# Inverses of 32x32 blocks: spread over partitions by VectorE's block transposes instead of through DRAM, in a bidirectional gated-DeltaNet encoder layer

## The chip, the cores and the metric

The kernel runs on one core of a Trainium2 chip. The metric is the device time of one execution in microseconds (us); lower is better. The kernel before took 1962.57 us, the median of three runs from 1961.55 to 1963.44.

## What is computed

One encoder layer over 16 learned ("meta") tokens and 1024 input tokens of width 1024, float32. A projection gives q, k, v, z and gates for eight heads. Branch A is a gated DeltaNet, run forward and backward in chunks; branch B is a short convolution. Both are gated, merged and projected, and a SwiGLU block follows. What matters here is the triangular system of each chunk, head and direction:

```
lmat = where(strict, beta[:, None] * (k @ k.T) * decay, 0)
a = lmat + eye
sol = triangular_solve(a, concat([v * beta, k * beta * exp(g)]), lower=True, unit_diagonal=True)
...
S = S * exp(g_last) + k_dec.T @ (u - w @ S)      # the scan over chunks
```

The kernel uses chunks of 128 tokens and builds the inverse of `a` itself: for each head 8 chunks in 2 directions, 16 matrices of 128x128. A small 16x16 system for the learned tokens comes on top.

## The kernel before, in words

**Stages.** The first stage (to about 985 us) does the input projection and, for each head, the whole DeltaNet branch. The second stage (from 985 us) does the other large products; the change does not touch it.

**Order in the first stage.** It is written out when the program is built. TensorE's main work are projection units: `dense_steps` (L332) multiplies 128 output columns by stretches of 320 to 512 tokens, 24 matmuls each, in groups of three. After each group `run_streams` and `pump` are called. They hold a simple clock for each engine (`T["pe"]`, `T["dve"]`, `T["act"]`, `T["pool"]`), to which `pe`, `V`, `A` and `on` add booked durations, for example `V(n)` = 68 + 1.042 n ns for VectorE and `A(n)` = 144 + 0.834 n ns for ScalarE. A stream is a Python generator that yields the time from which it may go on; it goes on when TensorE's clock has got there. So the pieces of the heads are put between the projection groups, and each engine then works its own instructions in this order. The streams of a head are `g_decay`, `g_norm` (norms of k and q, the scaled score matrices NP and PQ), `g_inv` (NP becomes its inverse) and `g_scan` (the recurrence over the chunks). Jobs of VectorE (convolutions, the substitution `fs_job`) lie in lanes that `pump` serves when VectorE's clock is free. `take` lets one of scan and inverse at a time use TensorE.

**The inverse, `g_inv`.** NP holds 16 matrices, chunk by chunk and direction by direction, rows on partitions. (1) The four 32x32 diagonal blocks `NP[B(b), c, d, B(b)]` are inverted by forward substitution, 64 blocks at once. For this each block shall lie in one partition row group: direction 1 is transposed in place (L639), the blocks are stored in DRAM (`nd`, L641) and loaded as `fN` (L653), one block row set per partition. `fP` starts as identity rows, GpSimd writes it. `fs_job` does 31 columns with two VectorE instructions each, a product into `tm` (L491) and a subtraction (L495). The result goes out to DRAM (`pd`, L671) and comes back into NP (L676). (2) Copies (L687 to L689) and transposes (L691 to L693, L697) prepare both forms of the inverted blocks, `X64` and `Xe`. (3) TensorE joins 32-wide blocks to 64-wide ones (L706, ScalarE's negated copy `T2` at L708, L714 and L716) and these to 128-wide ones (L729 and L730, `T3` at L732, L736 and L737).

**The learned tokens.** Their 16x16 matrix Nm (made in `g_norm`, L566 and L594) goes through DRAM to one partition (`mN`), GpSimd inverts it there (`mP`, L661 and L663) and the result goes through DRAM into `meta_inv` (L678), which the scan's first product uses.

**The scan's steps that are named below.** b1 and b2 are PSUM tiles: products with S (L796, L799), r from them on VectorE (L806), product with the inverse (L814), w on ScalarE (L821), state update S on VectorE (L841, L843).

**PSUM tiles.** Tag "m" (`psm`, 3 tiles) serves the projections, tag "e" (`psd`, 2 tiles) `g_norm`, tag "d" (`pss`, 3 tiles) inverse and scan. All DMAs of this stage are issued on SP's queue, in the order of the program.

Of the kernel before, what the change touches and what calls it, by code (L numbers as in the profile page):

```python
# [37 lines left out]
def encoder_layer(ctx: ExitStack, tc: tile.TileContext, x, meta, norm1_w, w_in,  # L38
# [183 lines left out]
    def pe(ns):  # L222
        T["pe"] += ns
        return T["pe"] + HOP
# [306 lines left out]
    def g_norm(h, st_):  # L531
# [90 lines left out]

    def g_inv(h, st_):

        NP, Nm = st_["NP"], st_["Nm"]

        nd = dr.tile([4, NC, 2, 32, 32], F32, tag="nd", name=uid("nd"), bufs=2)
        ndm = dr.tile([META, META], F32, tag="ndm", name=uid("ndm"), bufs=2)  # L630
        fN = dn.tile([P, 2, 512], F32, tag="fN", name=uid("fN")).rearrange("p a (j i) -> p (a j) i", i=32)
        fP = dn.tile([P, 16, 32], F32, tag="fP", name=uid("fP"))
        fPf = fP.rearrange("p j i -> p (j i)")
        mN = dn.tile([P, NC, 32], F32, tag="T2", name=uid("mN")).rearrange("p c i -> p (c i)")[:1]
        mPf = dn.tile([P, NC, 32], F32, tag="Xe", name=uid("mP")).rearrange("p c i -> p (c i)")[:1]
        mN, mP = (t.rearrange("p (j i) -> p j i", j=META) for t in (mN, mPf))
        nc.sync.dma_start(ndm, Nm)
        for b in range(4):
            nc.vector.transpose(NP[B(b), :, 1, B(b)], NP[B(b), :, 1, B(b)])  # L639
            on("dve", 467)  # L640
            nc.sync.dma_start(nd[b].rearrange("c d j i -> j (c d) i"),  # L641
                                             NP[B(b), :, :, B(b)].rearrange("j c d i -> j (c d) i"))
        nc.gpsimd.memset(fP, 0.0)
        nc.gpsimd.memset(fPf[0:64, 0:8 * 33:33], 1.0)
        nc.gpsimd.memset(fPf[0:64, 8 * 32 + 24:512:33], 1.0)
        nc.gpsimd.memset(fPf[64:128, 8:512:33], 1.0)
        nc.gpsimd.memset(mP, 0.0)
        nc.gpsimd.memset(mPf[:, 0:256:17], 1.0)
        on("pool", 500)
# [7 lines left out]
        for j in range(META - 1):  # L657
            n = META - 1 - j
            tm = dn.tile([1, 64], F32, tag="tmm", name=uid("tm"), bufs=1)
            tv = tm[:, :(j + 1) * n].rearrange("p (r i) -> p r i", r=j + 1)  # L660
            nc.gpsimd.tensor_tensor(out=tv, in0=mP[:, 0:j + 1, j:j + 1].broadcast_to([1, j + 1, n]),  # L661
                                    in1=mN[:, j:j + 1, j + 1:META].broadcast_to([1, j + 1, n]), op=ALU.mult)
            nc.gpsimd.tensor_tensor(out=mP[:, 0:j + 1, j + 1:META], in0=mP[:, 0:j + 1, j + 1:META], in1=tv,  # L663
                                    op=ALU.subtract)
            yield max(on("pool", 700) - TOPE, T["pe"] + 500)
        while not job.done:
            yield T["pe"] + 100
        yield T["dve"] + HOP
        pd = dr.tile([4, NC, 2, 32, 32], F32, tag="pd", name=uid("pd"), bufs=2)
        for r, src in (((0, 8), fP[0:64, 0:8]), ((24, 32), fP[0:64, 8:16]), ((8, 24), fP[64:128])):  # L670
            nc.sync.dma_start(pd[:, :, :, r[0]:r[1]].rearrange("b c d j i -> d (b c) (j i)"), src.rearrange("p j i -> p (j i)"))  # L671
# [1259 lines left out]
```

## Time and profile before

| | before |
|---|---|
| timed runs, median (lowest to highest) | 1962.57 us (1961.55 to 1963.44) |
| profiled execution: span from its first to its last instruction | 1959.4 us |
| time of the profiled execution around the span | not listed by itself; the median lies 3.2 us above the span |
| TensorE busy | 1941.7 us, 99% of the span |
| VectorE, ScalarE, GpSimd busy | 1468.1, 867.9, 158.4 us |
| mean granted TensorE clock | 0.999 |
| first stage, last projection matmul | near 985 us |

Busy time of TensorE comes from matmul records that overlap, with modelled ends, so 99% means that hardly a gap is seen, not that it runs at its peak. An instruction's name in the profile is line, engine, operation, output<-inputs and shape. Idle time carries the name of what ended it.

### The profile page before, as it was taken

To read this page: it belongs to the slowest core of one execution; us is meant where nothing else is said; L and a number is where in the kernel's file an instruction comes from. 1 tells how busy PE (TensorE), PEld (TensorE's weight loads), DVE (VectorE), ACT (ScalarE), POOL (GpSimd) and SP (SyncE) were. 2 spreads that over 40 slices of the span, in tenths; PEclk is the share of its full clock that TensorE was granted. 3 is DMA by queue.
4 is the path that set the end of the run, shared out by engine and by line. 5 is a ranking of instruction groups with operands and counts; after the bars stand their busy time and mean duration, and the time that the engine had idled before them with its cause. 6 is when DMAs were issued, how large, how long until landed. Compare 5 with 4: busy or idle time off the path is not lost.

```text
span 1959.4 us, 31938 instructions
## 1 busy us (share of the span) xinstructions
PE 1941.7 (99%) x11962; PEld 1704.4 (87%) x11962; DVE 1468.1 (75%) x2804; ACT 867.9 (44%) x2014; POOL 158.4 (8%) x457
## 2 busy tenths in 40 slices
PE   8999999999999999999999999999999999999998
PEld 8998899999899999998888888887888888888887
DVE  4778778788887888787358798559787887756574
ACT  5463544646455554533445545234232332324343
POOL 3012112020110202110000000000000000000001
PEclk9999999999999999999999999999999999999999
DMA  4222332323222222224386623332666644587654
GB/s 146 68 76 80 103 99 60 87 60 87 60 76 67 85 65 79 70 69 153 103 310 246 206 88 121 115 119 73 212 232 209 209 165 163 179 279 243 194 181 155
DMA packets 243136, 264.11 MB, mean 135 GB/s; under 512 B 46820, under 2 KB 166933, under 8 KB 240549
## 3 DMA queue, kind: packets, MB, share of 16 engines
q1 hardware_dynamic: 242981, 262.07, 42.1%
q8 instruction: 94, 1.54, 0.3%
q14 instruction: 61, 0.50, 0.1%
HBM read 189.58 MB, written 72.44 MB: 134 GB/s over the span
## 4 chain that ended last, share of the span: by engine, by line
PE 89%; DVE 5%; ACT 3%; issue 1%; DMA 1%; POOL 0%; SPq 0%; POOLq 0%; DVEq 0%; ACTq 0%
PE pm L332 31%; PE pm L1382 5%; PE pd L1382 4%; PE pe L1382 3%; PE pm L1656 3%; PE pm L1658 3%; PE pm L1657 2%; PE pd L1658 2%; PE pd L1656 2%; PE pd L1657 2%; PE pe L1658 2%; PE pe L1656 2%; PE pe L1657 2%; PE pm L1814 1%; PE pm L1815 1%; PE pm L1813 1%
## 5 line engine op out<-in xcount | busy, mean ns | idle before, releaser
L332 PE MATMUL pm<-hTh,wh 128*128 128x512 f32 (+4 forms) x1328 | 483.8, 365 | 0.1
L332 PE MATMUL pm<-hTh,wl 128*128 128x512 f32 (+4 forms) x1328 | 450.5, 340 | 0.0
L332 PE MATMUL pm<-al,wh 128*128 128x512 f32 (+4 forms) x1328 | 449.6, 339 | 0.5 <-DVE al L1047 0.5
L332 PEld LDWEIGHTS pm<-hTh,wl 128*128 128x128 f32 x1328 | 249.1, 188 | 15.5
L332 PEld LDWEIGHTS pm<-hTh,wh 128*128 128x128 f32 x1328 | 250.2, 189 | 13.6 <-ACT hTh L1041 0.2
L332 PEld LDWEIGHTS pm<-al,wh 128*128 128x128 f32 x1328 | 250.4, 189 | 12.9 <-DVE al L1047 0.7
L87 DVE TENSOR_TENSOR al<-raw,ring_h 128x1024 fp32r<-128x1024 f32 x73 | 88.4, 1223 | 63.6 <-ACT ring_h L86 63.2
L86 ACT CAST ring_h<-raw 128x1024 fp32r<-128x1024 f32 x73 | 76.9, 1054 | 109.7 <-PE pd L1815 35.3
L940 DVE TENSOR_TENSOR wl<-raw,wh 128x512 fp32r<-128x512 f32 x122 | 84.1, 690 | 32.0 <-ACT wh L943 27.1
L355 DVE SCALAR_TENSOR_TENSOR kq<-ra,wc,kq 128x520 f32<-128x520 f32 (+1 forms) x128 | 95.9, 749 | 2.3 <-ACT kq L389 1.2
L821 ACT ACTIVATE w<-pd,small 128x128 f32<-128x128 f32 x128 | 40.2, 365 | 124.9 <-PE pd L814 106.4
L128 POOL TENSOR_SCALAR ss<-ss 128x1 f32<-128x1 f32 x13 | 4.6, 353 | 951.1 <-ACT b L1825 603.4
L491 DVE TENSOR_TENSOR tm<-fP,fN 128x135 f32<-128x135 f32 (+23 forms) x248 | 72.1, 291 | 10.0 <-DMA fN<-nd 3.3
L495 DVE TENSOR_TENSOR fP<-fP,tm 128x135 f32<-128x135 f32 (+23 forms) x248 | 71.8, 289 | 7.3
L943 ACT CAST wh<-raw 128x512 fp32r<-128x512 f32 x122 | 74.8, 619 | 0.1
L87 DVE TENSOR_TENSOR raw<-pair,raw 128x1024 fp32r<-128x1024 f32 (+1 forms) x42 | 48.0, 1143 | 30.4 <-ACT raw L86 30.4
L86 ACT CAST raw<-pair 128x1024 fp32r<-128x1024 f32 (+1 forms) x42 | 41.7, 992 | 58.4 <-PE pd L1382 27.5
L87 DVE TENSOR_TENSOR wl<-pair,wh 128x1024 fp32r<-128x1024 f32 (+1 forms) x42 | 48.1, 1144 | 21.7 <-ACT wh L86 21.6
L86 ACT CAST wh<-pair 128x1024 fp32r<-128x1024 f32 (+1 forms) x42 | 41.7, 992 | 46.0 <-PE pd L1382 24.7
L843 DVE SCALAR_TENSOR_TENSOR S<-S,eGl,pd 128x128 f32<-128x128 f32 x104 | 31.8, 344 | 38.2 <-PE pd L831 30.8
L130 POOL TENSOR_TENSOR small<-small,minus_half 128x9 f32<-128x9 f32 x16 | 29.5, 1842 | 353.8 <-DVE small L878 264.0
L661 POOL TENSOR_TENSOR tm<-mP,mN 1x15 f32<-1x15 f32 (+7 forms) x120 | 37.3, 311 | 237.0 <-DMA mN<-ndm 228.7
(660 smaller groups left out, 4945.7 us busy)
## 6 DMA issues: line engine op xcount, KB each, us to landing
raw<-in_w_in_dram SPq DMA_DIRECT2D x64, 512.0 KB
raw<-in_w_gate_up_dram SPq DMA_DIRECT2D x44, 512.0 KB
sums<-in_w_down_dram SPq DMA_DIRECT2D x22, 512.0 KB
t_d<-sums SPq DMA_DIRECT2D x11, 1024.0 KB
raw<-s_d SPq DMA_DIRECT2D x44, 256.0 KB
raw<-t_d SPq DMA_DIRECT2D x44, 256.0 KB
act_d<-b SPq DMA_DIRECT2D x43, 256.0 KB
raw<-act_d SPq DMA_DIRECT2D x33, 256.0 KB
```

Source lines behind the costliest of these rows:

```text
L86: nc.scalar.copy(hi, src)
L87: nc.vector.tensor_tensor(out=lo, in0=src, in1=hi.bitcast(F32), op=ALU.subtract)
L332: mm(po[:, :n], (wl if j == 2 else wh)[:, k], xl[k][:, t0:t0 + n] if j == 1 else xh[k][:, t0:t0 + n], start=(i == 0), stop=(i == 3 * KT - 1))
L355: nc.vector.scalar_tensor_tensor(out=acc, in0=raw[:, h0 + t:h0 + t + hn], scalar=wc[:, t, col:col + 1], in1=acc, op0=ALU.mult, op1=ALU.add)
L491: nc.vector.tensor_tensor(out=tv, in0=fP[:, 0:r, j:j + 1].broadcast_to([P, r, n]), in1=fN[:, j:j + 1, j + 1:32].broadcast_to([P, r, n]), o ...
L495: nc.vector.tensor_tensor(out=fP[:, 0:r, j + 1:32], in0=fP[:, 0:r, j + 1:32], in1=tv, op=ALU.subtract)
L940: nc.vector.tensor_tensor(out=u[1][1][:, k], in0=u[2][:, k], in1=u[1][0][:, k].bitcast(F32), op=ALU.subtract)
L943: nc.scalar.copy(u[1][0][:, k], u[2][:, k])
L1382: mm(bank[t], a[:, c], b, start=fresh, stop=first and k == 3 and j == 2, skip_group_check=not first)
L1656: mm(po, ah[:, k], bhk, start=k == 0, stop=False)
L1657: mm(po, ah[:, k], blk, start=False, stop=False)
L1658: mm(po, al[:, k], bhk, start=False, stop=k == 3)
```

## The change

- **Spread.** ScalarE copies the four diagonal blocks of NP into a PSUM tile E of tag "e" (L657). VectorE transposes the 32x32 blocks of one direction in E (L660, 128x256), and then E as a whole into `fN` (L662, 128x1024, each block twice). No DRAM.
- **Substitution.** A partition now holds every second row of its block: `r = j // 2 + 1` rows are worked on at column j. GpSimd writes the new identity pattern with ten memsets.
- **Back.** VectorE transposes `fP` into Z (L674) and Z into W (L677), 128x512 each; they are both forms of the inverted blocks. TensorE's first products read them, and ScalarE copies the blocks into NP (`diag`) and `X64` later, between the products.
- **Learned tokens.** A stream of its own, `g_meta`, starts as soon as Nm is scaled. Nm (now with its sign turned) goes out to DRAM once and comes back to 16 partitions, all 16 rows in each; GpSimd then works one row of the inverse per partition, directly in `meta_inv`. The scan waits for `inverted` and `learned`.

The diff without the renaming in the third step:

```diff
@@ fs_job
-            r = min(j + 1, 8) if j < 16 else 8 + min(j - 15, 8)
+            r = j // 2 + 1
@@ g_norm
-        nc.vector.tensor_scalar(out=Nm, in0=Nm, scalar1=cc[:META, 8, 0:1], scalar2=None, op0=ALU.mult)
+        nc.vector.tensor_scalar(out=Nm, in0=Nm, scalar1=cc[:META, 8, 0:1], scalar2=-1.0, op0=ALU.mult, op1=ALU.mult)
         on("dve", 950)
+        st_["Nm_done"] = True
@@ new stream
+    def g_meta(h, st_):
+        Nm = st_["Nm"]
+        ndm = dr.tile([META, META], F32, tag="ndm", name=uid("ndm"), bufs=2)
+        mN = dn.tile([P, META, META], F32, tag="mN", name=uid("mN"))[:META]
+        nc.sync.dma_start(ndm, Nm)
+        yield T["dve"] + LAND
+        nc.sync.dma_start(mN, ndm.unsqueeze(0).broadcast_to([META, META, META]))
+        Pm = st_["Pm"] = meta_inv[h % 2]
+        mP = Pm[:META, :META]
+        nc.gpsimd.tensor_copy(mP, ident[:META, :META])
+        yield T["pe"] + 5600
+        for j in range(META - 1):
+            tm = dn.tile([META, META], F32, tag="tmm", name=uid("tm"))[:, j + 1:]
+            nc.gpsimd.tensor_scalar(out=tm, in0=mN[:, j, j + 1:], scalar1=mP[:, j:j + 1], scalar2=None, op0=ALU.mult)
+            nc.gpsimd.tensor_tensor(out=mP[:, j + 1:], in0=mP[:, j + 1:], in1=tm, op=ALU.add)
+            yield max(on("pool", 500) - TOPE, T["pe"] + 400)
@@ g_inv, spread
-        nc.sync.dma_start(ndm, Nm)
         for b in range(4):
-            nc.vector.transpose(NP[B(b), :, 1, B(b)], NP[B(b), :, 1, B(b)])
-            on("dve", 467)
-            nc.sync.dma_start(nd[b].rearrange("c d j i -> j (c d) i"), NP[B(b), :, :, B(b)].rearrange("j c d i -> j (c d) i"))
-        yield T["dve"] + LAND
-        for s in range(2):
-            for d in range(2):
-                nc.sync.dma_start(fN[64 * s + 32 * d:64 * s + 32 * d + 32], nd[:, :, d].rearrange("b c j i -> (b c) j i"))
-        nc.sync.dma_start(mN, ndm.unsqueeze(0))
-        yield T["pe"] + 5600
+            nc.scalar.copy(E[B(b)].rearrange("p d c i -> p c d i"), NP[B(b), :, :, B(b)])
+            A(512)
+        yield T["act"] + HOP
+        nc.vector.transpose(E[:, 0], E[:, 0])
+        yield V(256) - TOPE + DEP
+        nc.vector.transpose(fN.rearrange("p i (s x) -> p i s x", s=2),
+                            E.rearrange("p d c i -> p i (d c)").unsqueeze(2).broadcast_to([P, 32, 2, 2 * NC]))
+        yield V(1024) - TOPE + DEP
         job = enqueue("fs", fs_job(h, fN, fP))
-        ... (the learned tokens' 15 steps on one partition)
@@ g_inv, back
-        for r, src in (((0, 8), fP[0:64, 0:8]), ((24, 32), fP[0:64, 8:16]), ((8, 24), fP[64:128])):
-            nc.sync.dma_start(pd[...], src.rearrange("p j i -> p (j i)"))
-        nc.sync.dma_start(pdm.unsqueeze(0), mP)
-        yield T["dve"] + LAND
-        for b in range(4):
-            nc.sync.dma_start(NP[B(b), :, :, B(b)].rearrange("j c d i -> j (c d) i"), pd[b].rearrange("c d j i -> j (c d) i"))
-        nc.sync.dma_start(Pm[:META, :META], pdm)
-        yield T["pe"] + 5600
+        nc.vector.transpose(Z.rearrange("p d c r -> p r (d c)"), fP.rearrange("p r (s x) -> p (r s) x", s=2))
+        yield V(512) - TOPE + DEP
+        nc.vector.transpose(W, Z)
+        yield V(512) + HOP - TOPE
         yield from take("inv")
-        ... (three copies and seven transposes of 32x256)
+        def diag(d, b):
+            nc.scalar.copy(NP[B(b), :, d, B(b)], rows_[d][B(b), d])
+            A(256)
         ... (first products)
+        for d, b in ((0, 2), (0, 3), (1, 0), (1, 1)):
+            diag(d, b)
         yield t
         nc.scalar.mul(T2, pt, -1.0)
         ... (products with T2; after them four copies into X64, four from pp into NP as before, two diag)
         ... (64-wide products, T3, two diag, products with T3 as before)
@@ g_scan
-        while not st_.get("inverted"):
+        while not (st_.get("inverted") and st_.get("learned")):
```

Three places show what moves. Names end in buffer numbers: pe_, pd_ and pm_ are PSUM tiles of the tags "e", "d" and "m", kq_64 is head 1's k and q.

First, TensorE at the end of head 0's scores, where head 1's normalisation begins; before:

```order
L332 MATMUL pm_145_1533<-al_3_128,wh_118_1298 128x384
L332 MATMUL pm_145_1533<-hTh1_130,wl_119_1299 128x384
L83 MATMUL pe_155_1595<-ident_70,kq_64_896 128x128
L557 MATMUL pe_155_1595<-kq_64_896 128x16
L83 MATMUL pe_156_1598<-ident_70,kq_64_896 128x128 x4
L332 MATMUL pm_162_1614<-hTh0_129,wh_135_1443 128x512
```

And now:

```order
L332 MATMUL pm_151_1550<-al_3_128,wh_118_1298 128x384
L332 MATMUL pm_151_1550<-hTh1_130,wl_119_1299 128x384
L83 MATMUL pe_166_1632<-ident_70,kq_64_896 128x128
L557 MATMUL pe_166_1632<-kq_64_896 128x16
L83 MATMUL pe_167_1635<-ident_70,kq_64_896 128x128 x4
L332 MATMUL pm_174_1653<-hTh0_129,wh_137_1448 128x512
```

TensorE's order is the same, but between the last score tile and pe_166 a tile of the same tag, pe_160 (E), has been handed out.

Second, ScalarE at that place; before:

```order
L388 COPY ra_141_1492<-pm_142_1496 128x320
L389 ACTIVATE kq_123_1336<-pm_142_1496,wc_154 128x320
L561 COPY kn_154_1594<-pe_155_1595 128x128
L545 ACTIVATE jk_157_1604,small_153_1592<-pe_155_1595 16x128
L388 COPY ra_141_1492<-pm_145_1533 128x384
```

And now:

```order
L388 COPY ra_143_1497<-pm_144_1501 128x320
L389 ACTIVATE kq_123_1336<-pm_144_1501,wc_154 128x320
L657 COPY pe_160_1609<-NP_127_1353 32x8x2x32 x4
L561 COPY kn_165_1631<-pe_166_1632 128x128
L545 ACTIVATE jk_168_1641,small_164_1629<-pe_166_1632 16x128
L360 ACTIVATE rb_170_1645<-vT_65_897 128x520
```

The four copies into E stand ahead of the copy that reads pe_166.

Third, VectorE between head 0's substitution and its first products; before, after the trip through DRAM:

```order
L473 SCALAR_TENSOR_TENSOR rb_279_2284<-rb_279_2284,pm_275_2241 128x512
L363 SCALAR_TENSOR_TENSOR kq_123_1336<-rb_278_2276,kq_123_1336 128x520
L691 STREAM_TRANSPOSE XT_277_2260<-NP_127_1353 32x8x32
L692 STREAM_TRANSPOSE XT_277_2260<-NP_127_1353 32x8x32
L693 STREAM_TRANSPOSE Xe_276_2259<-NP_127_1353 32x256
L697 STREAM_TRANSPOSE NP_127_1353<-NP_127_1353 32x8x32 x4
```

And now, three instructions after the last substitution step:

```order
L495 TENSOR_TENSOR fP_162_1611<-fP_162_1611,tm_277_2191 128x16
L355 SCALAR_TENSOR_TENSOR kq_123_1336<-ra_125_1338,wc_154,kq_123_1336 128x520
L939 TENSOR_TENSOR wl_262_2131<-raw_236_1959,wh_261_2130 128x512
L674 STREAM_TRANSPOSE XT_278_2199<-fP_162_1611 128x32x16
L355 SCALAR_TENSOR_TENSOR kq_123_1336<-ra_125_1338,wc_154,kq_123_1336 128x520
L677 STREAM_TRANSPOSE W_283_2223<-XT_278_2199 128x512
```

Seven short transposes behind a DMA have become two long ones in a chain (the second reads what the first wrote), close behind the substitution.

More of the change, by code (lines that the diff above doesn't have):

```diff
@@ L654, in g_inv @@
-        nc.sync.dma_start(mN, ndm.unsqueeze(0))
-        yield T["pe"] + 5600
-        job = enqueue("fs", fs_job(h, fN, fP))
[L657 to L665, printed above, removed]
+        fPf = fP.rearrange("p r i -> p (r i)")
@@ L672, in g_inv @@
-        pdm = dr.tile([META, META], F32, tag="pdm", name=uid("pdm"), bufs=2)
-        nc.sync.dma_start(pdm.unsqueeze(0), mP)
-        yield T["dve"] + LAND
-        for b in range(4):
-            nc.sync.dma_start(NP[B(b), :, :, B(b)].rearrange("j c d i -> j (c d) i"), pd[b].rearrange("c d j i -> j (c d) i"))
-        Pm = st_["Pm"] = meta_inv[h % 2]
-        nc.sync.dma_start(Pm[:META, :META], pdm)
-        Xe = dn.tile([P, NC, 32], F32, tag="Xe", name=uid("Xe"))
         XT = dn.tile([P, 2, 512], F32, tag="fN", name=uid("XT"))
-        X64 = XT[:, 0].rearrange("p (c i) -> p c i", c=NC)
+        Z = XT[:, 0].rearrange("p (d c i) -> p d c i", d=2, c=NC)
@@ L955, in start_streams @@
             nnorm += 1
+        h = nmeta
+        if h < H and not metas and heads[h].get("Nm_done"):
+            metas.append([g_meta(h, heads[h]), T["dve"] + HOP, h])
+            nmeta += 1
         h = ninv
@@ L971, in run_streams @@
             again = False
-            for q in (scans, invs, norms, decs):
+            for q in (scans, invs, metas, norms, decs):
                 if q and q[0][1] <= T["pe"]:
```

93 lines of the change are left out of this document (42 added, 51 removed).

## The prediction

> **What bounds the kernel now.** I read the page first (busy shares), then the windows of the two stages, then TensorE's own waits, then the timeline around each of these waits. The first rows are the page's span and TensorE row, and two rows of the windows: columns are the stretch, its length, and busy time of PE, PEld, DVE, ACT and POOL, then the granted clock, the DMA share and GB/s.
>
> ```profile
> span 1959.4 us, 31938 instructions
> PE 1941.7 (99%) x11962; PEld 1704.4 (87%) x11962; DVE 1468.1 (75%) x2804; ACT 867.9 (44%) x2014; POOL 158.4 (8%) x457
> 100.00:900.00 800.00, 796.14 (x6554) 742.04 (x6553) 655.32 (x1707) 413.00 (x1322) 120.42 (x364) 1.00 0.29 78
> 985.00:1959.40 974.40, 965.69 (x4320) 799.55 (x4318) 712.53 (x895) 369.48 (x468) 15.61 (x33) 1.00 0.55 186
> ```
>
> TensorE is busy 796.14 of 800 us where all eight inversions run, at full clock. Every long step of a head is covered by projection matmuls (L332), which are put into the gaps. So the DRAM trips that the change removes cost nothing by their length: a head may wait 20 us and TensorE goes on. The change can gain only where TensorE itself stood still for an inversion, and lose only where it will. These are its waits (what, for whom: total us, times, longest):
>
> ```profile
> PE pd L714 <- ACT T L708: 1.7, 1, 1.7
> ...
> PE pd L796 <- DVE S L843: 0.6, 1, 0.6
> ...
> PE pd L814 <- DVE r L806: 0.5, 2, 0.3
> ...
> PE pd L729 <- POOL small L130: 0.4, 1, 0.4
> ```
>
> Idle time understates a wait, since a matmul's modelled end covers its first part. I take waits from starts instead: a matmul of 512 columns starts 0.23 us after the last, one of 384 columns 0.18 us, and the first small one of an interlude 0.32 us after a 512-column one when nothing is late (first two rows). The next rows are the same kind of place in other heads.
>
> ```profile
> 201.86 0.39 PE L332 MATMUL pm<-hTh,wl 128*128 128x512 f32 x1
> 202.18 0.21 PE L714 MATMUL pd<-NP,T 32*32 32x32 f32 x1
> ...
> 491.34 0.34 PE L332 MATMUL pm<-hTh,wl 128*128 128x384 f32 x1
> 493.35 0.21 PE L714 MATMUL pd<-NP,T 32*32 32x32 f32 x1 [1.67 <-ACT T L708]
> ...
> 702.99 0.34 PE L332 MATMUL pm<-hTh,wl 128*128 128x384 f32 x1
> 703.76 0.30 PE L729 MATMUL pd<-XT,NP 64*64 64x64 f32 x2 [0.43 <-POOL small L130]
> 704.21 0.24 PE L730 MATMUL pd<-XT,NP 64*64 64x64 f32 x1 [0.16 <-POOL fP L643]
> ...
> 233.45 0.40 PE L332 MATMUL pm<-hTh,wl 128*128 128x512 f32 x1
> 234.42 0.75 PE L796 MATMUL pd<-S,kq 128*128 128x128 f32 x4 [0.57 <-DVE S L843]
> ...
> 236.61 0.40 PE L332 MATMUL pm<-hTh,wl 128*128 128x512 f32 x1
> 237.32 0.71 PE L814 MATMUL pd<-r,NP 128*128 128x128 f32 x4 [0.32 <-DVE r L806]
> ```
>
> At 491 the step took 2.01 us against 0.27 (0.32 less the 0.05 by which 384 columns are shorter): 1.7 us lost. At 703 it is 0.77 - 0.27 = 0.5, and 0.4 more between L729 and L730, which start together elsewhere: 0.9. At 233 and 237 it is 0.97 - 0.23 = 0.74 and 0.71 - 0.23 = 0.48: 1.2. The first two (2.6 us) stand inside the inversion. The other two stand in a scan, and VectorE's timeline says why:
>
> ```profile
> 226.37 0.61 DVE L806 SCALAR_TENSOR_TENSOR r<-pd,negEG,vS 128x128 f32<-128x128 f32 x2 [1.46 <-PE pd L796]
> 230.28 0.22 DVE L491 TENSOR_TENSOR tm<-fP,fN 128x31 f32<-128x31 f32 x1 [3.30 <-DMA fN<-nd]
> ...
> 233.76 0.34 DVE L495 TENSOR_TENSOR fP<-fP,tm 128x135 f32<-128x135 f32 x1
> 234.03 0.59 DVE L843 SCALAR_TENSOR_TENSOR S<-S,eGl,pd 128x128 f32<-128x128 f32 x2
> ```
>
> VectorE stood 3.30 us in front of the first substitution step, because fN had not come back from DRAM. The scan's state update S (L843) queued behind it and came late, and with it the products that wait for S and r. This is the one place where the removed round trip reaches TensorE.
>
> **The change part by part.** *DMAs.* Of 19 transfers a head on SP's queue (Nm out, four nd, four fN, mN, three pd, pdm, four into NP, meta_inv) two stay, Nm out and a broadcast mN: 136 fewer in all. Nothing on TensorE waits for a DMA in this stage, so only the 1.2 us at 233 and 237 comes back, and weight loads behind them on SP come sooner, which nothing waits for.
>
> *VectorE.* Prices (mean ns of one is the number behind the comma):
>
> ```profile
> L697 DVE STREAM_TRANSPOSE NP<-NP 32x256 f32<-32x256 f32 x32 | 13.9, 435 | 1.2 <-ACT Xe L687 0.4
> L491 DVE TENSOR_TENSOR tm<-fP,fN 128x144 f32<-128x144 f32 x16 | 5.0, 310 | 0.4
> L491 DVE TENSOR_TENSOR tm<-fP,fN 128x16 f32<-128x16 f32 x8 | 1.5, 182 | 0.3
> L141 DVE TENSOR_TENSOR pair<-pair,pair 128x1024 f32<-128x1024 f32 x30 | 35.8, 1218 | 1.0 <-DMA pair<-in_w_branch_dn_dram 0.8
> ```
>
> An element costs (310 - 182) / 128 = 1.0 ns. The substitution keeps its 62 instructions a head, but r * n summed over the 31 columns falls from 3752 to 2856, so two passes save 1.8 us. Eleven transposes of 0.435 us (4.8 us) become four: 256 elements 0.44, 1024 elements 1.22, two of 512 at 0.70 (between the two rows), 3.1 us in all. Together 3.5 us a head, 28 us of the 655 above. VectorE is no bound; this is slack, and I book no time for it. No row shows a transpose that writes with a stride of 32 elements as the third one does: between 0.70 and, if such writes halve the rate, 1.4 us. I take 0.70 (the 32x256 rows lie on the same line as ordinary instructions) and keep 1.4 for the slow rival.
>
> *ScalarE.* It gains 13 instructions a head: four copies of 32x512 into PSUM, four of 32x256 into X64, eight of 32x256 back into NP, less three. By these rows that is 4 * 0.58 + 12 * 0.41 - 3 * 0.41 = 6.0 us a head, 48 on 413 busy of 800: room enough.
>
> ```profile
> L687 ACT COPY Xe<-NP 32x256 f32<-32x256 f32 x8 | 3.2, 406 | 9.5 <-DMA NP<-pd 6.4 <-DMA meta_inv<-pdm 3.0
> L739 ACT COPY NP<-pd 64x512 f32<-64x512 f32 x8 | 4.6, 581 | 14.3 <-PE pd L737 14.3
> ```
>
> *GpSimd* keeps 30 small instructions for the learned tokens and gets ten short memsets. They start earlier, in a job of their own, and end before the inverse; VectorE's first substitution step waits for the memsets. I book nothing; if the transfer of mN were as late as fN was at 230, the price would be that 1.2 us once.
>
> *TensorE* has the same matmuls, and the order shows as many interludes between projection matmuls (342 before, 343 after): no term.
>
> *The wait that is added.* The inversion's copy target E takes one of two PSUM tiles of the tag "e" from head 0's last score product until the second transpose. In that stretch head 1's normalisation starts: pe_166 gets the other tile, and the token transposes into the next tile (L83) must wait until ScalarE and VectorE have read pe_166. On ScalarE the four E copies stand ahead of this reading. The same place before:
>
> ```profile
> 130.63 0.27 PE L83 MATMUL pe<-ident,kq 128*128 128x128 f32 x1
> 130.74 0.29 PE L557 MATMUL pe<-kq 128*128 128x16 f32 x2
> 130.88 0.64 PE L83 MATMUL pe<-ident,kq 128*128 128x128 f32 x4
> ...
> 128.43 0.60 DVE L613 SCALAR_TENSOR_TENSOR NP<-pe,small,PQ 128x128 f32<-128x128 f32 x2
> ...
> 131.06 0.27 ACT L561 COPY kn<-pe 128x128 f32<-128x128 f32 x1 [4.23 <-PE pe L557]
> 131.23 0.26 ACT L545 ACTIVATE jk<-pe 16x128 f32<-16x128 f32 x1
> 131.40 0.18 ACT L545 ACTIVATION_READ_ACCUMULATOR jk<-pe 16x1 f32 x1
> ...
> 132.79 0.16 DVE L566 TENSOR_TENSOR Nm<-pe,Dm 16x16 f32<-16x16 f32 x1
> ```
>
> The last scores are written at 129.03 and the E copies can start there; ScalarE is idle for 4.23 us. Four of 0.58 that overlap a little end near 131.2. Then the copy of kn, the square with its reading (to about 131.7) and Nm (0.16 and a hand-over): the tile is free near 131.9, and TensorE, which started at 130.88, stands 1.0 us. Below, with ScalarE free when pe_166 is ready, the reading ends at 131.58 and Nm at 131.8: 0.9. Above, copies without overlap end at 131.5 and a projection step of VectorE stands in front of Nm: 1.6. I take 1.0, once.
>
> The Trainium skill (Perfetto Trace Analysis, Optimization Strategy) says that the same gap returning on the engine that should be saturated can mean that there is too little PSUM for the next tile. By it the gap would come in each of eight heads: 8.0 instead of 1.0 and a time near 1968. In the order I find matmuls into tag "e" only inside head 0's E; the trace of before, without E, has no such gap.
>
> *New steps on the inverse's way.* TensorE meets it four times a head as before (first products, products with T2, 64-wide products, products with T3). But the first now follow the substitution directly, behind two chained transposes, and on ScalarE copies stand ahead of T2 and T3. The planner books 601 ns for a 512-element transpose (68 + 1.042 * 512) where 0.70 us is to be expected, and 357 ns for a copy that takes 406: some 0.1 to 0.3 us late a head against a margin of 0.2 to 0.4. Before, six of eight heads lost nothing and two lost 1.7 and 0.9. Bounds: 0 a head, and 0.9 in each (7.2). I take 0.2 a head, 1.6, nearest to the six.
>
> **Sum.** -2.6 (inversion's waits) - 1.2 (fN late) + 1.0 (E) + 1.6 (new steps) = -1.2 us. The profiled span is 1959.4; the three timed runs lie around 1962.57, 3.2 above it, which I take as unchanged: 1961.4 us. The measurement tells about 0.2% (3.9 us) from no change, so this is "same", with a range of its own of 1959.5 to 1964.
>
> **Rivals.**
> 1. *Slower: the DRAM trips were slack.* The planner gave each trip 5.5 us and more, in which a late VectorE caught up. Now a late substitution hits TensorE at once, and if strided transposes take 1.4 us, the two make the first products 0.7 to 1.4 us late in every head. For it: the planner's price is under the rows. Against: TensorE's row shows scan steps that hang on VectorE with similar margins, and only 0.6 and 0.5 us of waits on them. At 1.4 a head: -3.8 + 1.0 + 11.2 = +8.4, 1971. It decides (+3.9) from 0.85 us a head. Chance 0.14. The E gap in every head (1968) has 0.03.
> 2. *Faster.* VectorE is 28 us freer and the new steps fit their margins: -3.8, only part of 1.0, and some small waits of the scans go too: 1958, from 1959 down to 1956.5. Against: TensorE's whole idle time in that stage is 3.9 us. Chance 0.15.
> 3. *Nothing moves*: the trips were covered, ScalarE's lateness at 491 comes back elsewhere as it does not hang on the inverse's transport: 1962.6. Chance 0.13.
>
> **Chances.** The forecast 0.55. Same by 0.2% holds it and the third rival, 0.68; faster 0.15, slower 0.17. The range reaches to the whole faster case and to the start of the slow one, where 0.14 is left out above and little below: 1957.5 to 1967.
>
> **What would show it.** No fN, nd or pd rows, and no DMA wait in front of L491; STREAM_TRANSPOSE x32 of four lengths, 512 elements at about 0.70 us; VectorE's busy time in 100 to 900 us near 627, ScalarE's near 460; one wait of about 1 us on TensorE near 131 us at L83 behind L566. Rival 1 would show waits at L692 on W in most heads; the tag "e" rule, a wait at L83 or L583 in each. I am wrong if the waits at L692, L703, L725 and L735 add up to over 6 us, or if the scans' waits go altogether.

## The result, and the profile after

The changed kernel takes 1983.95 us (median, 1983.25 to 1983.99), the kernel before 1963.01 us on the same chip: 1.0107 times as long, with a 95% interval from 1.0092 to 1.0121. I had forecast 1961.4. The change costs 21 us, and TensorE's instruction count is what it was.

The page of the changed kernel, and the windows' row that answers to the 796.14 of before:

```profile
span 1982.3 us, 31711 instructions
PE 1948.3 (98%) x11962; PEld 1708.7 (86%) x11962; DVE 1440.5 (73%) x2748; ACT 913.0 (46%) x2118; POOL 167.5 (8%) x497
100.00:900.00 800.00, 779.99 (x6463) 727.52 (x6462) 618.60 (x1637) 456.26 (x1423) 129.56 (x404) 0.99 0.21 63
```

VectorE's and ScalarE's totals came out near the forecast (618.6 against 627, 456.3 against 460), yet TensorE is busy for 16 us less of the same 800. The first stage's last projection matmul (L332) starts at 1007.2 us instead of 985.2, and the rest of the program takes 975.1 us against 974.2: almost all of the loss lies in the first stage. Its waits there (what, for whom: total us, times, longest):

```profile
PE pe L83 <- DVE Nm L566: 9.4, 5, 6.2
PE pd L692 <- DVE XT L674: 2.7, 1, 2.7
PE pd L692 <- DVE W L677: 1.8, 2, 0.9
PE pd L813 <- DVE r L805: 1.7, 2, 1.0
PE pd L83 <- DVE NP L898: 1.5, 1, 1.5
...
PE pd L795 <- DVE S L784: 0.8, 1, 0.8
PE pd L703 <- issue: 0.6, 1, 0.6
PE pd L726 <- ACT XT L708: 0.5, 1, 0.5
```

Measured from starts as in the prediction (each interlude, that is, what stands between two projection groups, against the shortest of its kind; places over 0.06 us), before loses 10.4 us in 35 places and the changed kernel 29.0 in 46. I call this sum "lost in waits" below. It is a guide and no exact account: it leaves out projection matmuls that run at a slow clock, and it can miss a wait in an interlude that has no second one of its kind. Here it explains 18.6 of the 22 us. Two places hold 11 us, 131 (6.7) and 491 (4.3); the others have at most 1.7.

**At 131 us.** This is the place where I had forecast one wait of 1.0 us behind E. The timeline, of GpSimd (POOL), ScalarE and TensorE:

```profile
131.97 0.26 ACT L561 COPY kn<-pe 128x128 f32<-128x128 f32 x1
132.12 0.30 POOL L638 TENSOR_SCALAR tm<-mN,meta_inv 16x8 f32<-16x8 f32 x1
...
134.67 0.51 POOL L649 MEMSET fP<- 128x512 f32 x1
...
136.81 0.18 POOL L539 MEMSET small<- 128x108 f32 x1
...
137.02 0.27 ACT L545 ACTIVATE jk<-pe 16x128 f32<-16x128 f32 x1 [4.80 <-POOL small L539]
...
137.53 0.16 DVE L566 TENSOR_TENSOR Nm<-pe,Dm 16x16 f32<-16x16 f32 x1 [5.96 <-ACT jk L545]
...
137.75 1.11 PE L83 MATMUL pe<-ident,kq 128*128 128x128 f32 x4 [6.18 <-DVE Nm L566]
```

Read from the bottom: TensorE waits for Nm, Nm (on VectorE) for the square, the square (on ScalarE, 4.80 us) for a memset of head 1's "small". That memset is GpSimd's, and it stands behind head 0's learned-token steps and fP's ten memsets. Before, the same L539 ran at 124.86. A pair of steps is booked with 500 ns; in the trace head 0's follow each other at 0.66 to 1.31 us, and at 2.14 where fP's memsets come between.

The wait has a second price. In the windows of this stretch the number behind POOL's busy time is the granted clock:

```profile
134.00:136.00 2.00, 0.00 (x0) 0.00 (x0) 0.00 (x0) 0.00 (x0) 1.62 (x11) 1.00 0.00 0
136.00:138.00 2.00, 0.25 (x1) 0.26 (x2) 0.47 (x2) 0.97 (x4) 1.54 (x8) 0.61 0.00 0
138.00:140.00 2.00, 2.00 (x8) 1.60 (x8) 1.97 (x4) 0.86 (x3) 0.65 (x3) 0.50 0.00 0
142.00:144.00 2.00, 2.00 (x12) 1.74 (x11) 0.00 (x0) 0.88 (x3) 0.00 (x0) 0.68 0.00 0
144.00:146.00 2.00, 2.00 (x13) 1.69 (x12) 0.00 (x0) 1.85 (x9) 0.00 (x0) 1.00 0.00 0
```

TensorE comes back at half its clock and keeps it for some 5.5 us; a 512-column matmul takes 0.43 us from start to start there instead of 0.23, and about 2.5 us more are lost (an estimate from these steps).

**At 491 us** the substitution ends late and the first products wait for both transposes:

```profile
488.80 0.16 DVE L566 TENSOR_TENSOR Nm<-pe,Dm 16x16 f32<-16x16 f32 x1 [3.26 <-ACT jk L545]
...
492.66 1.04 DVE L674 STREAM_TRANSPOSE XT<-fP 128x512 f32<-128x512 f32 x1
...
493.75 0.25 PE L692 MATMUL pd<-XT,NP 32*32 32x32 f32 x4 [2.74 <-DVE XT L674]
494.16 0.69 DVE L677 STREAM_TRANSPOSE W<-XT 128x512 f32<-128x512 f32 x1
...
494.91 0.26 PE L692 MATMUL pd<-W,NP 32*32 32x32 f32 x2 [0.91 <-DVE W L677]
```

VectorE had stood 3.26 us in front of Nm of the head after, which waited for ScalarE, and the last substitution steps stood behind Nm.

**At 388 us** ScalarE's queue shows plainly. A block of the inverse's copies stands ahead of the next head's kn:

```profile
385.10 0.81 ACT L708 COPY XT<-XT 32x256 f32<-32x256 f32 x2
...
385.93 0.81 ACT L708 COPY XT<-W 32x256 f32<-32x256 f32 x2
...
386.76 1.49 ACT L715 COPY NP<-pd 32x256 f32<-32x256 f32 x4
...
388.26 0.81 ACT L686 COPY NP<-XT 32x256 f32<-32x256 f32 x2
389.10 0.27 ACT L561 COPY kn<-pe 128x128 f32<-128x128 f32 x1
...
389.98 0.65 PE L83 MATMUL pe<-ident,kq 128*128 128x128 f32 x4 [1.31 <-DVE Nm L566]
```

### The profile page after: what moved, and what is told of

Same layout as the page of the kernel before. It is cut to its first block, busy times and chain, and to the rows that moved or that the text cites. A ratio compares the mean times of both kernels' runs of the same rounds, so it can differ in the third digit from the quotient of the medians.

```text
span 1982.3 us, 31711 instructions
## 1 busy us (share of the span) xinstructions
PE 1948.3 (98%) x11962; PEld 1708.7 (86%) x11962; DVE 1440.5 (73%) x2748; ACT 913.0 (46%) x2118; POOL 167.5 (8%) x497
## 4 chain that ended last, share of the span: by engine, by line
PE 81%; DVE 9%; ACT 6%; issue 1%; DMA 1%; POOL 1%; SPq 0%; POOLq 0%; ACTq 0%; DVEq 0%
PE pm L332 26%; PE pm L1385 4%; PE pd L1385 4%; PE pe L1385 3%; PE pm L1659 2%; PE pm L1661 2%; PE pm L1660 2%; PE pd L1661 2%; PE pd L1660 2%; PE pd L1659 2%; PE pe L1661 2%; PE pe L1660 2%; PE pe L1659 2%; PE pm L1817 1%; PE pm L1818 1%
## 5 line engine op out<-in xcount | busy, mean ns | idle before, releaser
L332 PE MATMUL pm<-hTh,wh 128*128 128x512 f32 (+4 forms) x1328 | 485.5, 366 | 0.1
L332 PE MATMUL pm<-hTh,wl 128*128 128x512 f32 (+4 forms) x1328 | 451.0, 340 | 0.0
L332 PE MATMUL pm<-al,wh 128*128 128x512 f32 (+4 forms) x1328 | 450.2, 340 | 0.5 <-DVE al L1050 0.5
L332 PEld LDWEIGHTS pm<-hTh,wl 128*128 128x128 f32 x1328 | 249.8, 188 | 15.7
L332 PEld LDWEIGHTS pm<-hTh,wh 128*128 128x128 f32 x1328 | 250.9, 189 | 13.6 <-ACT hTh L1044 0.2
L332 PEld LDWEIGHTS pm<-al,wh 128*128 128x128 f32 x1328 | 251.1, 189 | 13.1 <-DVE al L1050 0.7
L355 DVE SCALAR_TENSOR_TENSOR kq<-ra,wc,kq 128x520 f32<-128x520 f32 (+1 forms) x128 | 95.7, 748 | 1.4
L128 POOL TENSOR_SCALAR ss<-ss 128x1 f32<-128x1 f32 x13 | 4.6, 350 | 975.1 <-ACT b L1828 603.4
L495 DVE TENSOR_TENSOR fP<-fP,tm 128x126 f32<-128x126 f32 (+22 forms) x248 | 62.8, 253 | 6.9
L491 DVE TENSOR_TENSOR tm<-fP,fN 128x126 f32<-128x126 f32 (+22 forms) x248 | 62.8, 253 | 6.7
L870 ACT ACTIVATE jk<-NP 128x128 f32<-128x128 f32 x64 | 19.9, 310 | 82.5 <-DVE NP L866 82.1
```

Source lines behind the costliest of these rows:

```text
L332: mm(po[:, :n], (wl if j == 2 else wh)[:, k], xl[k][:, t0:t0 + n] if j == 1 else xh[k][:, t0:t0 + n], start=(i == 0), stop=(i == 3 * KT - 1))
L355: nc.vector.scalar_tensor_tensor(out=acc, in0=raw[:, h0 + t:h0 + t + hn], scalar=wc[:, t, col:col + 1], in1=acc, op0=ALU.mult, op1=ALU.add)
L491: nc.vector.tensor_tensor(out=tv, in0=fP[:, 0:r, j:j + 1].broadcast_to([P, r, n]), in1=fN[:, j:j + 1, j + 1:32].broadcast_to([P, r, n]), o ...
L495: nc.vector.tensor_tensor(out=fP[:, 0:r, j + 1:32], in0=fP[:, 0:r, j + 1:32], in1=tv, op=ALU.subtract)
```

## The experiments

Each row is one kernel: its median, its ratio to the kernel before on the same chip with the interval, where its last L332 starts, and what it lost in waits. The last two columns are read from the one profiled execution, which can lie some us from the median (e8's took 1981.8).

| kernel | us | ratio | last L332 | lost |
|---|---|---|---|---|
| before (first chip) | 1963.0 | 1 | 985.2 | 10.4 |
| changed | 1984.0 | 1.0107 [1.0092, 1.0121] | 1007.2 | 29.0 |
| e1 small by VectorE | 1977.7 | 1.0078 [1.0063, 1.0093] | 999.8 | 23.3 |
| e2 learned tokens only | 1966.5 | 1.0020 [1.0011, 1.0029] | 989.9 | 13.3 |
| e4 blocks only | 1978.1 | 1.0077 [1.0060, 1.0094] | 1002.6 | 24.3 |
| e3 e1 + measured prices | 1971.6 | 1.0045 [1.0030, 1.0060] | 994.1 | 17.2 |
| e5 e3 + E copies one by one | 1979.6 | 1.0091 [1.0076, 1.0106] | 1001.4 | 21.0 |
| e6 e3 + T2 first | 1979.2 | 1.0090 [1.0075, 1.0105] | 1000.8 | 21.5 |
| e7 e5 + e6 + E in tag d | 1975.2 | 1.0071 [1.0054, 1.0087] | 997.5 | 19.6 |
| e8 e3 + diagonals on VectorE | 1978.0 | 1.0088 [1.0073, 1.0103] | 1004.2 | 20.6 |
| d1 e1 without diagonals | 1972.2 | 1.0052 [1.0037, 1.0067] | 994.8 | 17.7 |
| d3 e1, contiguous | 1976.5 | 1.0079 [1.0063, 1.0096] | 999.3 | 21.0 |
| d4 d1 + d3 | 1970.5 | 1.0046 [1.0031, 1.0061] | 993.7 | 16.3 |
| v1 e1, half of E on VectorE | 1986.1 | 1.0126 [1.0109, 1.0143] | 1009.8 | 30.6 |
| s1 e3 + slack | 1967.1 | 1.0027 [1.0016, 1.0038] | 990.5 | 12.0 |
| s3 s1 without diagonals | 1964.6 | 1.0014 [1.0005, 1.0024] | 988.0 | 10.6 |
| s2 s1 + T2 first, tag d | 1969.8 | 1.0040 [1.0025, 1.0055] | 993.5 | 16.7 |
| p1 before, LAND 5300 | 1959.0 | 0.9985 [0.9975, 0.9994] | 984.5 | 9.4 |
| p3 before, LAND 5700 | 1957.7 | 0.9980 [0.9971, 0.9989] | 981.0 | 6.0 |
| p5 before, LAND 6500 | 1959.9 | 0.9991 [0.9982, 1.0001] | 983.8 | 7.2 |

**GpSimd's queue (e1, e2, e4).** e1 moves one memset:

```
-        nc.gpsimd.memset(small, 1.0)
+        nc.vector.memset(small, 1.0)
```

> The changed kernel with one memset moved: 'small' of each head (L539) is set by VectorE instead of GpSimd. Theory A (GpSimd's queue): at 131 us ScalarE's square (L545) stood 4.80 us for this memset, which was queued behind the learned tokens' 30 steps and the ten memsets of fP; TensorE stood 6.7 us, and then ran some 5 us at a granted clock of 0.50 (another 2.5 us). Then the wait at L83 near 131 us shrinks to about 1.3 us, the slow clock there goes, and the time falls by 7 to 9 us, to about 1976. Rival B (ScalarE's four E copies hold the tile, the memset was only the last to come): the wait stays above 4 us and the time above 1981. Neither touches the stall of 4.3 us at 491.

6.3 us faster, a little less than the 7 to 9 of theory A, with every other instruction where it stood. At 131 1.4 us are lost instead of 6.7, and the slow clock there is gone. The row for all five heads falls from 9.4 us, longest 6.2, to

```profile
PE pe L83 <- DVE Nm L566: 4.5, 5, 1.4
```

So GpSimd's queue carries 6.3 of the 21 us, and the wait that the prediction gave E is 1.4. (One gap grew, from 0.6 to 2.0 us, near 270; it is explained under e3.) e2 and e4 apply one half of the change each: e2 is g_meta with its job (L627 to L640) on the old g_inv, e4 the new g_inv with the old one-partition steps.

> The kernel before with the learned tokens' part of the change alone (own job, one row per partition on GpSimd; its row of mN is kept as a packed triangle to fit the memory, in two DMAs); the blocks go through DRAM as before. Theory A: the steps stand in GpSimd's queue ahead of the next head's memset of 'small' here too, so head 1's L83 waits several us and the time rises by 5 to 9 us, to 1968 to 1972. If the learned tokens' part only hurts together with the fP memsets and the E copies, the time stays at 1962 to 1964 and the blocks' part carries the 21 us.

> The changed kernel's blocks (E, block transposes, new substitution) with the learned tokens as before: one partition, inside the inversion's job, through DRAM and back. Theory A: no GpSimd steps run beside the next head's normalisation, so no long wait near 131 us: 1972 to 1977. Theory C and D: the waits of the inversion and of the scans are there as in the changed kernel, 8 to 12 us above the kernel before. If the blocks' part is harmless by itself, 1962 to 1964.

e2 costs about 4 us (theory A said 5 to 9): its only new wait of weight is L83 at 133, 3.4 us lost, behind the same memset at 135.53, and its clock, too, is at 0.50 behind it (136.2 to 139.6 us). e4 costs 15.5 us, above what any theory expected, and has no long wait at 131 (1.4 us lost). The two halves add up to 19.5 of the 21 us, but each half is also a new order of the instructions, which by itself moves the time (e5 to e8 below), so the sum proves little.

**What the planner books (e3), and its order (e5 to e8).**

```
-            A(512)                              # E copies, 571
+            on("act", 605)
-        yield V(512) - TOPE + DEP               # L674, 601
+        yield on("dve", 1040) - TOPE + DEP
```

and the other new instructions likewise.

> As the run with the memset on VectorE, and the planner's prices of the change's new instructions set to what the trace shows: E copies 605 ns (571 were booked), VectorE's transposes 450, 1250, 1040 and 700 ns (335, 1135, 601, 601 booked), copies of 32x256 405 ns (357 booked). Theory C (booked too short: the new steps reach TensorE late, worst at 491 where the strided transpose of 1.04 us precedes the first products): the waits at L692 to L726 shrink and most of the 12 us that are left after the memset come back: 1964 to 1968. Rival D (ScalarE's queue has 6 us a head more, whatever is booked, and the next head's small copies and squares stand behind it): 1972 to 1976, the waits at L83 behind L566 stay.

6.1 us faster, some 40% of what was left after e1; neither theory had the size. The loss at 491 is gone. But the new prices also give the planner a new order, so the 6.1 us can't be put down to the prices alone. A wait of 2.7 us near 268 stays. I took it for ScalarE's, since T2 (L697) stands behind the four diagonal copies there, and e6 below was built on that reading. The rows say otherwise:

```profile
266.08 0.38 ACT L697 ACTIVATE T<-pd 128x256 f32<-128x256 f32 x1
...
266.94 0.21 PE L703 MATMUL pd<-W,T 32*32 32x32 f32 x1
...
267.58 0.19 PE L703 MATMUL pd<-W,T 32*32 32x32 f32 x1
270.48 0.18 PE L705 MATMUL pd<-T,W 32*32 32x32 f32 x1 [2.70 <-issue]
```

The products start once T2 is there and then stop in the middle of the group. "issue" means that no semaphore or DMA of the program ended the wait. In the trace a 16 KB transfer on the DMA queue that the page calls "instruction" runs from 268.07 to 269.07, and TensorE goes on 1.4 us after its end. Ten of the traces (changed, e1, e3, e4, e6, e8, v1, d1, d3, d4) have this gap, of 0.6 to 4.7 us, after exactly the same number of TensorE instructions, 3777, and each ends 1.3 to 1.4 us after such a transfer. In e8 it is a projection matmul that stands there, which needs no T2:

```profile
PE pm L332 <- issue: 4.7, 1, 4.7
```

So I read this gap as TensorE waiting for its own next instructions; no run changes that transfer alone. In e3 two groups of small products come before it (L692, and most of L703 and L705), 279 matmuls and weight loads in the 4.2 us from 263.41 to 267.58. In the kernel before, the instruction at that count starts 19 us after its transfer has landed, and nothing waits. The clock can fall behind it as well: e3's is 0.50 from 271.5 to 274.9 us. Why the transfer comes so late isn't shown; the DMA engines were busy 99% of the 4.4 us ahead of it in e3, but only 54% in e4.

e5 to e8 go at such places, as I read them, one by one: a yield after each E copy; the four L686 put behind T2; both, with head 0's E in tag d; the eight L686 on VectorE.

> As the run with the measured prices, and the four E copies handed to ScalarE one at a time, so that the scan's own small steps can go between them. Theory E (the block of 2.42 us stands in ScalarE's queue ahead of the scan's L860, and TensorE waits at L813 for r, 1.5 us at 435 and 1.1 us at 527): these waits go, about 2.5 us, to 1969. Rival D (it is ScalarE's total load): the waits move but their sum stays, 1971 to 1972.

> As the run with the measured prices, and the first four diagonal copies (L686) put behind T2 (L697) in ScalarE's queue instead of ahead of it. Theory F (the copies hold T2 up whenever ScalarE is behind: at 266 TensorE stood 2.7 us in front of L703 to L705): that wait goes, 2 to 2.5 us, to 1969. If the booked order already covers the copies elsewhere, only this one place changes. Rival D: the copies then hold up what comes next (NP copies, the next head's kn) and the time stays at 1971 to 1972.

> Both of these edits, and head 0's E in a PSUM tile of tag d instead of e. Theories E and F add up, and the wait of 1.4 us at 131 (head 1's token transposes behind E) falls to the 0.3 us of before: 1965.5. If the places depend on each other, 1968 to 1970. Under 1962 it would beat the kernel before; I do not expect it.

> As the run with the measured prices, and the eight diagonal copies (L686, 3.2 us a head) moved from ScalarE to VectorE, which the change had relieved by about as much. Rival D (ScalarE's load): 3 to 6 us faster, 1966 to 1968, with smaller waits at L83 behind L566 and at L703. Theory F alone: 2 us faster, at 266. If VectorE's queue is as tight, the waits come back at L692 and L813 and the time stays or rises.

All four missed, and on the wrong side: 3.6 to 8 us slower than e3. Each edit gives the planner a new order, and the losses came up in other places (e5: 2.7 us at 135, where L83 now waits for ScalarE's square, 2.4 at 606 in front of L583 and 2.3 at 404; e6: still 3.0 at 263; e8: 4.7 at 265, 3.6 at 481 and 3.3 at 841). e6's and e8's gaps at 263 and 265 are the instruction gap, so theory F had the wrong cause there. On the rest of their theories they say nothing, so from here on I changed work under an unchanged order, or changed the order alone.

**Work taken away under the same order (d1, d3, d4, v1).**

```
 def diag(d, b):                                 # d1: booked, not issued
-    nc.scalar.copy(NP[B(b), :, d, B(b)], rows_[d][B(b), d])
+    pass
     A(256)
...
-nc.vector.transpose(Z.rearrange("p d c r -> p r (d c)"), fP...)   # d3: L674
+nc.vector.transpose(XT[:, 0], fPf)
...
+(nc.vector.tensor_copy if b > 1 else nc.scalar.copy)(E[B(b)]...)  # v1: L657
```

> The changed kernel with VectorE's memset (1977.7) without the eight diagonal copies (L686, 0.40 us each, 26 us of ScalarE in all); NP keeps the blocks' negative products there. They are still booked, so that every other instruction stands where it stood. Theory D (ScalarE's load): the waits at L703 (266), L83 (380, 578) and L726 (377) go, 4 to 6 us, to 1972 to 1974. If ScalarE's queue is not what these places wait for, under 1.5 us.

5.5 us faster than e1. Loss fell from 2.2 to 0.9 us at 266, from 1.0 to nothing and 1.5 to 0.6 at 377 to 380, from 1.6 to 0.4 at 706; at 578 it fell only from 1.6 to 1.4, and at 482 it stayed at 4.2. At 266 it is the instruction gap that shrank (2.0 to 0.7 us), which isn't shown to be ScalarE's doing. So 3.2 us a head of short copies, on an engine that is busy 57% of this stretch, cost 0.5 to 0.7 us a head.

> The changed kernel with VectorE's memset (1977.7), and the first transpose back (L674) written contiguously instead of with a stride, so that its blocks land in the wrong places; everything else stands where it stood. It took 1.04 us against 0.69 for the contiguous one behind it. If the strided write is what makes the inverse late, the waits at L692 shrink by 0.35 us where they are seen (482, 367, 880): 1 us at most, 1976.7. If the 4.1 us at 482 come from the substitution itself being late (VectorE waits behind Nm and ScalarE there), nearly all of it stays.

> Both edits that take work away in one: no diagonal copies (booked all the same) and the contiguous transpose. If the two are independent, 1972.2 less what the contiguous one alone gives, 1971. What is then left above 1962 (9 us) belongs to the E copies, the planner's order and the direct chain, since neither of these edits changes the order.

The stride costs what the durations say (1.04 against 0.69 us), 0.4 of the 4.1 us at 482; the 1.2 and 1.7 us by which these two medians are lower lie well inside the ranges of these runs (4.4 and 4.2 us from lowest to highest). At 482 it was the late substitution, not the transpose.

> The changed kernel with the memset on VectorE (1977.7), and two of the four E copies of each head moved from ScalarE to VectorE, in the same order otherwise. If the E copies on ScalarE hold up the scan behind them (L813 at 249 and 323) and head 1's kn at 130, these three waits of 1.0, 1.3 and 1.4 us shrink by about half, 1.5 to 2 us, to 1976. If the waits for r come from VectorE's own queue, they stay or grow: 1978 to 1980.

8.4 us slower: VectorE's queue has no more room than ScalarE's. The two copies take 1.4 us a head there (0.70 each), and the waits for r and S grew, where I had expected them to shrink or to cost 2 us at most:

```profile
PE pd L813 <- DVE r L805: 3.5, 5, 1.1
PE pd L703 <- issue: 3.2, 1, 3.2
...
PE pd L795 <- DVE S L842: 1.4, 3, 0.9
```

The 8.4 us are not all VectorE's: the second row is the instruction gap, 1.2 us longer than in e1, and the clock is at 0.50 for 13.7 us of this trace's first stage, against 3.4 in e1's. At 130 the wait grew too (2.6 us lost), since the memset now stood behind the E copies on VectorE. That ScalarE's E copies cause the waits at 249 and 323 is therefore not shown.

**The order alone, and the slack (p1, p3, s1, s3, s2, p5).**

> The kernel before, with the same instructions and one number of its planner changed: a DRAM trip is booked with 5300 ns instead of 5500 (LAND). Some 15% of the rows of each engine's order move. Theory G (the order of before is a rare good draw: any other order of this plan puts small waits of about the same sum elsewhere, so part of what is left of the changed kernel's loss is the new draw and not its work): 1966 to 1975. Theory H (the loss belongs to the new work): 1961 to 1964.

> As the run before it, with a DRAM trip booked at 5700 ns. Theory G: again above 1966, at other places. Theory H: 1961 to 1964, since later times are only more careful.

Theory G, as far as it says that the order of before is a rare good draw, is out: both other orders are a little faster, below the range of theory H too. That part of the changed kernel's loss is a matter of its own order is not out; with the same work e3 and e5 are 8 us apart. p3 loses nothing inside the inversion; its row of the windows:

```profile
100.00:900.00 800.00, 799.16 (x6578) 744.90 (x6577) 659.72 (x1707) 415.13 (x1326) 121.22 (x364) 1.00 0.28 79
```

s1 puts the trips' booked time into e3 as plain waiting:

```
-        yield on("dve", 1250) - TOPE + DEP
+        on("dve", 1250)
+        yield T["dve"] + LAND
+        yield T["pe"] + 5600
```

(behind L662, and the same behind L677).

> The changed kernel with VectorE's memset and the measured prices (1971.6), and the planner made to leave the slack that the DRAM trips had: 5500 ns after the transposes into fN and before the first products, and 5600 ns of TensorE's time behind each. Rival 1 of the prediction (a late substitution now hits TensorE at once, since the trips' slack is gone): 1964 to 1967, no waits at L692. If the waits belong to ScalarE's queue (L83 behind L566, L813 behind r), they stay and the time is 1969 to 1974.

> The run with the trips' slack given back (1967.1) without the diagonal copies, which are booked all the same; NP keeps the blocks' negative products there. If ScalarE's load still costs there (386 at L83, 660 at L817, 711 at L583), 2 to 4 us: 1963 to 1965, near the kernel before. If slack alone had taken that cost away, 1966 to 1967, and what is left belongs to E at 131 and to VectorE.

s1 is 4.4 us faster than e3, just above the range for rival 1, and at the first products (L692, in s1 and s3 L696) it holds no wait for a transpose (one of 0.9 us is for vS of ScalarE). But s1 is a new order as well, and e3's instruction gap (2.7 us, with the slow clock behind it) is gone in it: other instructions stand at that count. So how much of the 4.4 us the slack itself is worth isn't shown. s3 keeps s1's order, has no such gap either, and is 2.5 us faster again; the wait of 1.0 at 386 stays, so that one isn't the diagonals'. The waits of s3 in the first stage (its lines L799 and L817 are L795 and L813 elsewhere):

```profile
PE pe L83 <- DVE Nm L566: 2.3, 2, 1.3
PE pd L817 <- DVE r L809: 2.0, 3, 1.5
...
PE pe L83 <- ACT jk L545: 1.1, 2, 0.8
PE pd L696 <- ACT vS L767: 0.9, 1, 0.9
PE pd L799 <- DVE S L846: 0.8, 1, 0.8
```

> The run with the trips' slack given back (1967.1), with T2 ahead of the diagonal copies and head 0's E in a tile of tag d. The wait of 1.4 us at 131 goes to 0.3 or to the 0.8 that the run of three edits showed; the others are a new order's. With slack the order is tolerant, so 1964 to 1967. If edits to the order cost as much here as they did without slack (4 to 8 us), 1971 or more.

> The kernel before with a DRAM trip booked at 6500 ns instead of 5500. 5700 gave 1957.7 without a wait inside the inversion. If slack for the inversion is what TensorE needs, 1956 to 1959 again. If that run was luck of the order, 1959 to 1964.

s2 took away the wait at 131, but its new order costs 2.7 us against s1, more than expected and less than the 8 of e5 and e6. p5 came out at 1959.9, in the range that I had given to luck of the order, so p3's gain isn't shown to be slack. All three other orders of the kernel before lie between 1957.7 and 1959.9. No version of the changed kernel reaches the kernel before; p3, which has none of the change, is the fastest, 0.2% below it (interval 0.1 to 0.3%).

## Why the prediction was wrong, step by step

- **GpSimd, booked at nothing: this step failed first.** I asked who waits for the learned tokens' result and for fP, and not which instruction of another head stands behind them in GpSimd's queue. It was a memset of 0.18 us. Price: 6.3 us (e1), of which the clock's share is about 2.5 in the trace.
- **ScalarE, "48 on 413 busy of 800: room enough": failed.** The load was right (456) and the conclusion wrong. I followed the copies only to T2 and T3, and left out kn and the squares of the next head, which share the queue. Price: 5.5 us for the diagonals alone (d1), of which 1.3 are the instruction gap's; 2.5 in s1's order (s3).
- **New steps, 0.2 us a head, 1.6: mis-sized.** The four places lost about 7 us in all, most of it at 491, which is over the 6 us that I had named as a sign of being wrong. I took the planner's under-booking for 0.1 to 0.3 us at each step, and did not ask what else on the same in-order queue a late step delays. With the measured prices 6.1 us come back (e3), but in a new order, so this isn't a price of the under-booking alone.
- **Rival 1 (the trips were slack, chance 0.14) had the right mechanism at 491.** It named the late substitution and the short prices. In the traces the first products follow the last substitution step (L495) by 18.9 to 23.9 us before, and by 1.7 to 5.2 us now in seven of eight heads, 1.7 at 491; there a late VectorE reaches TensorE at once. What the slack is worth over all heads is not shown: waiting as long as the trips did (s1) gives 4.4 us back on top of e3, but in a new order and without the instruction gap. Rival 1 priced the inverse's products only; more than half of the loss fell on waits of other work, L83, L813 and L795. "TensorE goes on while a head waits 20 us" was true, and it is why the trips cost nothing; that they could also keep late engines away from TensorE I gave one rival, with too small a chance.
- **E: right.** 1.0 us at 131 behind L566, bounds 0.9 to 1.6; 1.4 measured once the memset is out of the way, and none in s2, where head 0's E is a tile of tag d. The rule that the gap would return in every head did not hold for E: at 388, where the wait at L83 behind L566 comes back, no E is held (E copies ran at 326 and 440), and ScalarE's queue is what is late.
- **fN late, -1.2: the waits at 233 and 237 went**, but scans lost 1.0 to 1.3 us at 257, 331 and 714 instead.
- **VectorE:** 0.70 us for the contiguous transpose was right (0.68 to 0.71). The strided one took 1.04 to 1.15, inside the bounds of 0.70 and 1.4; I chose the low end. It matters little (d3).
- **TensorE's own instructions: not in the prediction at all.** Its *TensorE* paragraph counts matmuls and interludes and books no term. The instruction gap costs 0.6 us in the changed kernel and up to 4.7 in its variants, and nothing in before.

About 3 us remain between s3 and the kernel before, and the waits at 249 and 323 have no shown cause.

## What to carry to other kernels

Where a static order feeds in-order queues, price a moved instruction by what stands behind it in its queue, of every head, and not by its engine's busy share: a 0.18 us memset on an engine 8% busy cost 6 us. A long transfer that is fully covered may still serve as slack in which late engines catch up; before removing it, book the replacements at their measured durations and ask what absorbs lateness afterwards. When testing causes in such a kernel, change the work and keep the order: edits that re-plan moved the time by 4 to 8 us for reasons of their own. And before naming the engine behind a wait, look where in the group it lies and what ended it: a gap inside a group of small matmuls that ends with "issue" was not the input's.

## What the hardware showed that I had not expected

**The clock.** The granted clock fell to 0.50 at about 136.5 us, 4.9 us after TensorE's last matmul, and was back at about 143.3, 5.5 us after it resumed; at 495 us it fell 3.8 us after the last projection matmul, with four small matmuls between, and was back 3.3 us after work resumed. Waits of up to 1.7 us in this trace did not touch it. The two slow stretches last 6.8 and 3.4 us. The Trainium skill (TensorE: Matmul & The Clock Gate, Part 1) says that the clock is halved after an idle window of about 3.4 us and returns after about as much sustained work, by a free-running window. These rows agree with it within 2.1 us.

**TensorE's instructions.** The gap shown under e3 lies at one place of TensorE's stream in ten traces and ends 1.3 to 1.4 us after a 16 KB transfer on the queue called "instruction". It cost up to 4.7 us.

**GpSimd beside VectorE.** GpSimd's small steps depend on what VectorE does. Here L639 runs once beside VectorE's L614, once beside its L355, and later with VectorE idle (132 to 137 us):

```profile
128.97 0.60 DVE L614 SCALAR_TENSOR_TENSOR NP<-pe,small,PQ 128x128 f32<-128x128 f32 x2
...
129.29 0.20 POOL L639 TENSOR_TENSOR meta_inv<-meta_inv,tm 16x11 f32<-16x11 f32 x1
...
129.95 0.75 DVE L355 SCALAR_TENSOR_TENSOR vT<-ra,wc,vT 128x520 f32<-128x520 f32 x1
...
129.98 0.77 POOL L639 TENSOR_TENSOR meta_inv<-meta_inv,tm 16x10 f32<-16x10 f32 x1
...
133.19 0.19 POOL L639 TENSOR_TENSOR meta_inv<-meta_inv,tm 16x7 f32<-16x7 f32 x1
```

L355 reads two large operands from SBUF (ra, vT), L614 one from PSUM (pe) and one from SBUF; only L355 stretched the step, to its own length. The Trainium skill (GPSIMD Engine Reference, Specifications) says that GpSimd's SBUF interfaces are shared with VectorE and contend with its instructions that have two SBUF inputs; these three rows agree. It made the learned tokens' pairs, and with them the memset at 131, later still.
